# The gate of a decoder layer as seven block products per pair of tiles, its weight sums and the embedding product made during the up projection

## The chip, the cores and the metric

One core of a Trainium2 chip. The metric is the device time of one execution in microseconds; the median of three runs of the kernel before is 2149.36 us (2148.55 to 2155.91).

## The reference, cut to what matters

One layer over a prompt of 2048 rows and a sample group of 64 rows, D = 1024, all in float32. After the mixer come the feed-forward part and the gate:

```python
hf = rmsnorm(x, g_pre_mlp)
ff = jnp.square(jax.nn.relu(hf @ w_up)) @ w_down       # 1024 -> 4096 -> 1024
x = x + rmsnorm(ff, g_post_mlp)
gate = jax.nn.sigmoid(x @ w_ple_gate + b_ple_gate)     # 1024 -> 1024
x = x + gate * (pe @ w_ple)                            # pe: 256 columns per row
```

The change is in the last two lines and in where their parts are made.

## The kernel before, in words

Rows are worked on in 16 tiles of 128 (t = 0 to 15) and one of 64 for the sample group (t = -1). Each float32 operand of a product is split in two parts of a narrower float type, the high part by a cast on ACT and the low part as the difference on VectorE (`split_into`, L205 to L208, `lo_of`, L129), and each product of 128 x 128 by 128 x 512 is three matmuls: high by high, high by low, low by high (`mm3`, L132).

Four stages follow one another, and TensorE goes through them in this order:

1. The mixer (attention, pooling, output projection), to about 610 us; it also writes the first residual's rows to DRAM (`x1d`).
2. The up projection, to about 1267 us. Rows are taken in pairs of tiles, which makes a product of 2 x 2 blocks, done by Strassen's scheme in Winograd's form: seven block products in place of eight (`UpQuad`: p1, p2, p6, p7, p5 and two in `end`). Sums of blocks of the rows and of the weights are formed first (`a_sums`, L848; `up_weights`, L1004). 3 blocks of 352 columns by 16 slices of the weights are 48 rounds; `ahead` (L1150) loads and splits the weights of the next round. In block 0 VectorE also forms the weight differences, which go to DRAM (`upt`) for the other two blocks.
3. The down projection (`down_quads`, L1368), to about 1903 us: 8 groups of weights by 8 pairs of tiles, again seven products each; the sums of rows and weights are made on GpSimd, and the products are added on VectorE to 17 tiles `zs` that stay in SBUF. In the last group the places for weights that come free take the first of the gate's weights.
4. The gate, tile by tile (`gate`, L1447; the order is 0, 1, the sample, 2 to 15). `second_residual` (L1201) of the tile after: the sum of squares on ACT, two one-column operations on GpSimd, scaling and addition of `x1d` on VectorE, eight transposes on TensorE into a PSUM bank, split out of that bank. Then for each half of 512 columns 8 block products (24 matmuls) with the split gate weights that lie in SBUF and 2 (6 matmuls) of the embedding. The end of a half:

```python
V.tensor_tensor(out=y, in0=pg[:n], in1=bgate[:n, oc], op=ALU.add)
A.activation(out=y, in_=y, func=AF.Tanh, scale=0.5)
V.scalar_tensor_tensor(out=y, in0=y, scalar=1.0, in1=pl[:n, cs], op0=ALU.add, op1=ALU.mult)
V.scalar_tensor_tensor(out=y, in0=y, scalar=0.5, in1=zs[t][:n, oc], op0=ALU.mult, op1=ALU.add)
SY.dma_start(yr[:, oc], y)
```

`pg` and `pl` are PSUM banks. The last half of the last tile is done in two pieces of 256 columns, so that less is left after the last matmul.

The order of the instructions of each engine is fixed when the kernel is built: a scheduler takes them in the order of the program, lets one go ahead of another by what it reckons of their times, and each engine then runs its own list in order. `products` (L945) sets the order of the program in stages 2 and 3: p1 of a pair, then the last two products (`end`) of the pair before, then p2, p6, p7, p5; `ahead` and `then` hang other work on these steps. All transfers are issued from one queue, SP's, in order. PSUM has six banks for products (`acc`) and two for transposes (`trb`). Tiles in SBUF come from rings of places: `raws` (4 and one more, 4 KB a partition), `wr` (10, 8 KB), `turned8` (3, 8 KB).

Of the kernel before, what the change touches and what calls it, by code (L numbers as in the profile page):

```python
# [51 lines left out]
UP_N = 352  # L52

# [35 lines left out]
def trunk(ctx: ExitStack, tc: tile.TileContext, i: dict, o: dict):  # L89
# [728 lines left out]
    with ExitStack() as sb:  # L818
# [27 lines left out]
        x1d = {t: dp.tile([P, D], F32, name=f"x1d{t + 1}") for t in range(-1, NT)}  # L846

# [118 lines left out]
        with ExitStack() as s3:  # L966
# [36 lines left out]

            def up_weights(b, j):  # L1004
# [105 lines left out]
            def up_rounds():  # L1110
# [36 lines left out]
                for k, r in enumerate(rounds):  # L1147
                    quads = [UpQuad(*r[0], o7s[r[0][0]], held.pop(k))]

                    def ahead(k=k, b=r[-1][0], j=r[-1][1]):  # L1150
                        begin(1) if k == 0 else prepare(k + 1)
                        if j == DFF // 256 - 2 and b + 1 < N_BLOCKS:
                            o7s[b + 1] = load_ops(b + 1)
# [13 lines left out]
        zs = {t: zp.tile([P, D], F32, name=f"z{t + 1}") for t in range(-1, NT)}  # L1167
# [12 lines left out]
        def gate_unit(load):  # L1180
            raw = raws.tile([P, 2, 512], F32)
            queue(raw, load.rearrange("(k p) f -> p k f", p=P))
            return wtile(raw)

        wgs, wps = {}, {}

        def gate_weights():

            for nh in range(2):
                ns = slice(nh * 512, nh * 512 + 512)  # L1190
                for u in range(4):
                    wgs[u, nh] = gate_unit(w_gate[u * 256 : (u + 1) * 256, ns])
                    yield
                wps[nh] = gate_unit(w_ple[:, ns])
                yield

        gate_loads = gate_weights()

        gpost = None

        def second_residual(t):  # L1201

            m = turned8.tile([P, 2, 8, P], F32R)
            n = tn(t)
            z = zs[t]
            xt = raws.tile([P, D], F32)
            SY.dma_start(xt[:n], x1d[t][:n])
            rs = sumsq(few, z[:n], n, m.rearrange("p a c n -> p (a c n)")[:, :D])
            V.scalar_tensor_tensor(out=z[:n], in0=z[:n], scalar=rs[:n], in1=gpost[:n], op0=ALU.mult, op1=ALU.mult)
            V.tensor_tensor(out=z[:n], in0=xt[:n], in1=z[:n], op=ALU.add)  # L1210
            for j in range(2):
                ps = trb.tile([P, 4, P], F32, tag="tr", name="trx")
                for c in range(4):
                    T.transpose(ps[:, c, :n], z[:n, (4 * j + c) * P : (4 * j + c + 1) * P], ident[:n, :n])
                js = slice(4 * j, 4 * j + 4)
                lo = m[:, 1, js] if t >= 0 else m[:, 0, js, NS:]
                A.copy(out=m[:, 0, js, :n], in_=ps[:, :, :n])
                lo_of(lo, ps[:, :, :n], m[:, 0, js, :n])
            return m

        with ExitStack() as s4:
# [48 lines left out]
            class DownQuad:  # L1270
# [51 lines left out]
                def end(self):  # L1322
# [3 lines left out]
                    self.add(self.z, 1, 0)  # L1326

# [40 lines left out]
            def down_quads():  # L1368
# [4 lines left out]
                def quad(k):  # L1373
# [3 lines left out]
                    def ahead():  # L1377
# [15 lines left out]
                        else:  # L1393
# [3 lines left out]
                            if 2 <= tp <= 4:  # L1397
                                next(gate_loads)
                            if tp == 3:
                                fold_sample()  # L1400

# [14 lines left out]
                def more(k, tile=None):  # L1416
                    for _ in islice(gate_loads, k):
                        pass
                    if tile is not None:
                        normed[tile] = second_residual(tile)  # L1420

                r.then = {"p2": lambda: more(2, 0), "p6": lambda: more(1), "p7": lambda: more(1), "p5": lambda: more(1)}
                yield [q, r]

            normed = {}
# [3 lines left out]
        with ExitStack() as s5:  # L1429
            p5 = pool(s5, "p5")  # L1430

            def embedding(t):
                n = tn(t)
                c0 = t * P if t >= 0 else SEQ
                pt = p5.tile([P, 2, P], F32, tag="pt", bufs=2, name="pt")
                SY.dma_start(pt[:, :, :n], p_t[:, :, c0 : c0 + n])
                pe = p5.tile([P, 2, 2, P], F32R, tag="pe", bufs=2, name="pe")
# [95 lines left out]
```

## Time and profile before

| | |
|---|---|
| runs, us | 2148.55, 2155.91, 2149.36 |
| span of the profiled execution, us | 2152.2 |
| device time of that very execution | not listed apart from the runs |
| granted TensorE clock, mean | 0.994 |
| matmuls in the program | 11439 |
| moved by DMA | 320.43 MB, 149 GB/s over the span |

How to read the profile: PE is TensorE's matmuls, PEld its weight loads, DVE VectorE, ACT ScalarE, POOL GpSimd, SP the engine that issues transfers. A group of instructions is shown by line, engine, operation, output and inputs and their shapes; then the count, its busy time, the mean in ns, the idle time of the engine just before it and what ended that. A row of the timeline begins with start and duration in us. Matmuls of a stream overlap in the records: the duration of one is longer than the distance to the next.

### The profile page before, as it was taken

The numbers are of one execution on the slowest core, as the hardware profiler recorded it, in microseconds if no ns is written. First come the engines' busy times: TensorE is split into PE (matmuls) and PEld (weight loads), VectorE is DVE, ScalarE is ACT, GpSimd is POOL, SyncE is SP. The second block draws the span as 40 slices with busy tenths as digits, with TensorE's granted clock in tenths as the row PEclk, the third lists the DMA queues.
The fourth block names the chain that finished last, engine by engine and source line by source line (L and its number), as shares of the span: only waits on it lengthen the run. The fifth ranks groups of instructions, "written<-read, shape, count | busy, mean of one in ns | idle before, by whom it ended". The sixth has DMA issues, their size and how long they took to land.

```text
span 2152.2 us, 31209 instructions
## 1 busy us (share of the span) xinstructions
PE 2130.7 (99%) x11439; PEld 1884.6 (88%) x11439; DVE 1572.5 (73%) x2719; ACT 958.2 (45%) x1864; POOL 569.4 (26%) x643
## 2 busy tenths in 40 slices
PE   8999999999999999999999999999999999999999
PEld 6888888788889999999999988888888888888887
DVE  6799888876678777555755577888888888876553
ACT  4667666545555446444544455232233233232221
POOL 2334334343440000000000046434434444300000
PEclk9999999999999999999999999999999999999999
DMA  7552222768789768666766632231231322342211
GB/s 219 169 184 80 75 62 74 265 216 235 237 248 315 239 216 276 203 191 191 229 194 187 182 112 78 91 121 51 93 96 53 98 93 71 106 138 83 89 54 40
DMA packets 310007, 320.43 MB, mean 149 GB/s; under 512 B 79775, under 2 KB 257247, under 8 KB 302654
## 3 DMA queue, kind: packets, MB, share of 16 engines
q1 hardware_dynamic: 309854, 318.44, 47.1%
q8 instruction: 90, 1.47, 0.3%
q14 instruction: 63, 0.52, 0.1%
HBM read 217.17 MB, written 102.51 MB: 149 GB/s over the span
## 4 chain that ended last, share of the span: by engine, by line
PE 90%; DMA 3%; POOL 2%; issue 2%; ACT 2%; DVE 2%; SPq 0%; ACTq 0%; POOLq 0%; DVEq 0%
PE up L1056 10%; PE up L1058 10%; PE up L1057 10%; PE dn L1289 9%; PE dn L1287 9%; PE dn L1288 9%; PE pg L136 3%; PE pg L135 3%; PE pg L134 3%; PE qps L136 1%; PE ups L134 1%; PE qps L134 1%; PE ups L136 1%; PE ups L135 1%; PE qps L135 1%
## 5 line engine op out<-in xcount | busy, mean ns | idle before, releaser
L1297 DVE TENSOR_TENSOR z<-dn,z 128x512 f32<-128x512 f32 x416 | 280.4, 685 | 86.1 <-PE dn L1289 78.9
L130 DVE TENSOR_TENSOR g<-raw,g 128x512 fp32r<-128x512 f32 x336 | 226.1, 694 | 82.9 <-ACT g L207 82.4
L1056 PE MATMUL up<-e,g 128*128 128x352 f32 x832 | 269.4, 324 | 5.4 <-ACT snap L1063 5.4
L1057 PE MATMUL up<-e,g 128*128 128x352 f32 x832 | 267.9, 322 | 0.0
L1058 PE MATMUL up<-e,g 128*128 128x352 f32 x832 | 264.0, 323 | 0.0
L207 ACT CAST g<-raw 128x512 fp32r<-128x512 f32 x336 | 203.2, 623 | 90.1 <-PE up L1058 80.8
L1236 POOL TENSOR_TENSOR raws<-raws 128x1024 f32<-128x1024 f32 x32 | 80.0, 2504 | 595.7 <-DVE wr L130 407.9
L1288 PE MATMUL dn<-wr,ms 128*128 128x512 f32 x512 | 199.2, 389 | 0.0
L1287 PE MATMUL dn<-wr,ms 128*128 128x512 f32 x512 | 199.1, 389 | 0.0
L1289 PE MATMUL dn<-wr,ms 128*128 128x512 f32 x512 | 198.2, 389 | 0.0
L1056 PEld LDWEIGHTS up<-e,g 128*128 128x128 f32 x832 | 156.6, 188 | 6.6 <-ACT snap L1063 6.5
L1070 DVE TENSOR_TENSOR t<-up,snap 128x352 f32<-128x352 f32 x144 | 71.2, 520 | 120.3 <-ACT snap L1063 101.8
L1057 PEld LDWEIGHTS up<-e,g 128*128 128x128 f32 x832 | 157.4, 189 | 0.1
L1058 PEld LDWEIGHTS up<-e,g 128*128 128x128 f32 x832 | 156.0, 189 | 0.0
L1288 PE MATMUL dn<-wr,m 128*128 128x512 f32 x384 | 149.4, 389 | 0.0
L1287 PE MATMUL dn<-wr,m 128*128 128x512 f32 x384 | 149.4, 389 | 0.0
L1289 PE MATMUL dn<-wr,m 128*128 128x512 f32 x384 | 149.4, 389 | 0.0
L207 ACT CAST m<-fr 128x512 fp32r<-128x512 f32 (+1 forms) x128 | 65.5, 514 | 185.2 <-PE dn L1289 167.6
L1063 ACT COPY snap<-up 128x352 f32<-128x352 f32 x144 | 61.0, 455 | 175.0 <-PE up L1058 174.9
L849 POOL TENSOR_TENSOR s<-fr 128x256 f32<-128x256 f32 x64 | 49.5, 774 | 334.7 <-DVE ms L130 252.8
L207 ACT CAST wr<-raws 128x1024 fp32r<-128x1024 f32 x66 | 69.1, 1051 | 122.8 <-PE dn L1289 58.8
L141 POOL TENSOR_SCALAR rst<-ss 128x1 f32<-128x1 f32 (+1 forms) x68 | 25.3, 372 | 340.1 <-ACT ms L183 211.4
(279 smaller groups left out, 5798.8 us busy)
## 6 DMA issues: line engine op xcount, KB each, us to landing
raw<-in_w_up_dram SPq DMA_DIRECT2D x160, 256.0 KB, 5.0
raw<-upt SPq DMA_DIRECT2D x32, 1024.0 KB, 7.8
fr<-ffd SPq DMA_DIRECT2D x64, 512.0 KB, 3.6
ffd<-r SPq DMA_DIRECT2D x96, 256.0 KB, 2.6
upt<-raw SPq DMA_DIRECT2D x16, 1024.0 KB
raws<-in_w_down_dram SPq DMA_DIRECT2D x32, 512.0 KB, 5.5
sp<-hfd SPq DMA_DIRECT2D x21, 704.0 KB, 6.5
xt<-in_x_t_dram SPq DMA_DIRECT2D x16, 512.0 KB, 7.2
```

The source lines that it names most:

```text
L130: eng.tensor_tensor(out=out, in0=full, in1=hi.bitcast(F32), op=ALU.subtract)
L134: T.matmul(ps, lhs[0], rhs[0], start=first, stop=False)
L135: T.matmul(ps, lhs[0], rhs[1], start=False, stop=False)
L136: T.matmul(ps, lhs[1], rhs[0], start=False, stop=last)
L207: copy(out=dst[:, 0], in_=src)
L1056: T.matmul(ps, l[0], r[0], start=st, stop=False, skip_group_check=not fresh)
L1057: T.matmul(ps, l[0], r[1], start=False, stop=False, skip_group_check=not fresh)
L1058: T.matmul(ps, l[1], r[0], start=False, stop=c == 3, skip_group_check=not fresh)
L1287: T.matmul(ps, l[0], r[0], start=fresh and j == 0, stop=False, skip_group_check=not fresh)
L1288: T.matmul(ps, l[0], r[1], start=False, stop=False, skip_group_check=not fresh)
L1289: T.matmul(ps, l[1], r[0], start=False, stop=j == 1, skip_group_check=not fresh)
L1297: V.tensor_tensor(out=z, in0=ps, in1=z, op=ALU.add)
```

## The change

- **The gate** goes by pairs of tiles, seven block products of 4 x 3 matmuls each (`GateQuad`), in the order of pairs 0, 6, 7, 1, 2, 3, 4, 5; the sample (`GateSample`) comes second, with four products of block rows as before. `products` sets the order here as well. The sums of a pair's blocks are made on GpSimd (`gate_sum_operands`), and the first and third partial sums are copied out of PSUM on ACT and get the bias on GpSimd (`snap`).
- **The gate's weights**: four differences, formed on GpSimd, and seven splits of them are made during the up projection (`gate_sums`) and go to DRAM as `gwd`; 14 loads of 1 MB bring them back, from the last down group on.
- **The embedding product** with its factor 0.5 is also made during the up projection (`embeddings`), into the banks of `trb`, and goes to DRAM (`pld`); the gate reads it from SBUF.
- `ahead` of the up projection takes two steps of these two (`aside`) in every round after round 2.
- **The rows**: the 16 tiles `zs` become a ring `zr` of eight pairs. Pairs 1 to 5 are written to DRAM (`zd`) when their last down product is added, and their places take gate weights and row sums; they come back one by one in the gate (`load`). The addition of the first residual moves to GpSimd, but for the pair 6; its rows from `x1d` go through one place of `raws` for both tiles.

The diff, cut:

```diff
+SPILLED = (1, 2, 3, 4, 5)
+GATE_ORDER = (0, 6, 7, 1, 2, 3, 4, 5)
...
+            def gate_sums(st):
+                gw = pool(st, "gw")
+                for c in range(4):
+                    raw = gw.tile([P, 7, 512], F32, tag="raw", bufs=1, name="graw")
+                    b11, b21, t2, t3, t1, b22, t4 = (raw[:, k] for k in range(7))
+                    for dst, r, h in ((b11, 0, 0), (t3, 0, 1), (b22, 1, 1), (b21, 1, 0)):
+                        SY.dma_start(dst, w_gate[r * 512 + c * P : r * 512 + c * P + P, h * 512 : h * 512 + 512])
+                    yield
+                    for t, x, y in ((t1, t3, b11), (t2, b22, t1), (t3, b22, t3), (t4, b21, t2)):
+                        G.tensor_tensor(out=t, in0=x, in1=y, op=ALU.subtract)
+                    yield
+                    for k in range(7):
+                        w = gw.tile([P, 2, 512], F32R, tag="w", bufs=1, name="gw")
+                        split_into(w, raw[:, k], A.copy)
+                        yield
+                        SY.dma_start(gwd[k][c // 2][:, :, c % 2], w.bitcast(F32))
...
+                    ps = trb.tile([P, 512], F32, tag="tr", name="pl")
+                    for c in range(2):
+                        mm3(ps[:n], (pe[:, 0, c, :n], pe[:, 1, c, :n]), (w[:, 0, c], w[:, 1, c]), c == 0, c == 1)
+                    out[k] = ep.tile([P, 512], F32, tag="pl", bufs=2, name="plo")
+                    A.mul(out=out[k][:n], in_=ps[:n], mul=0.5)
+                    store(k - 1)
+                    yield
...
                         begin(1) if k == 0 else prepare(k + 1)
+                        for _ in islice(aside, 2 if k > 2 else 0):
+                            pass
...
+        def second_rows(t, junk, add=G, xt=None):
             n = tn(t)
             z = zs[t]
+            if xt is None:
+                xt = first_rows(t)
+            rs = sumsq(few, z[:n], n, junk)
             V.scalar_tensor_tensor(out=z[:n], in0=z[:n], scalar=rs[:n], in1=gpost[:n], op0=ALU.mult, op1=ALU.mult)
-            V.tensor_tensor(out=z[:n], in0=xt[:n], in1=z[:n], op=ALU.add)
+            add.tensor_tensor(out=z[:n], in0=xt[:n], in1=z[:n], op=ALU.add)
...
+        def gate_sum_operands(tp, h, s, s23, s14, a22):
+            (a11, a12), (a21, b22) = halves(h[0]), halves(h[1])
+            s1, s2 = next(s), next(s)
+            G.tensor_tensor(out=s1, in0=a21, in1=b22, op=ALU.add)
+            G.tensor_tensor(out=s2, in0=s1, in1=a11, op=ALU.subtract)
+            split_into(s23[:, :, 0:4], s2, A.copy)
+            split_into(s14[:, :, 0:4], s1, A.copy)
+            s3 = next(s)
+            G.tensor_tensor(out=s3, in0=a11, in1=a21, op=ALU.subtract)
+            split_into(s23[:, :, 4:8], s3, A.copy)
+            G.tensor_tensor(out=s2, in0=a12, in1=s2, op=ALU.subtract)
+            split_into(s14[:, :, 4:8], s2, A.copy)
+            a22 = a22()
+            split_into(a22, b22, A.copy)
...
+                    if self.g == DFF // 512 - 1 and self.tp in SPILLED:
+                        SY.dma_start(zd[self.tp], pair_rows[self.tp])
...
+                def snap(self, ps):
+                    s = self.place()
+                    with tc.high_priority():
+                        A.copy(out=s, in_=ps)
+                    G.tensor_tensor(out=s, in0=s, in1=self.bias(0), op=ALU.add)
+                    return s
+                def plus(self, out, ps, s):
+                    with tc.high_priority():
+                        V.tensor_tensor(out=out, in0=ps, in1=s, op=ALU.add)
+                def out(self, h, c, y, cs=slice(0, 512)):
...
+                    A.activation(out=y, in_=y, func=AF.Tanh, scale=0.5)
+                    V.scalar_tensor_tensor(out=y, in0=y, scalar=1.0, in1=self.pl[h ^ c][:, h, cs], op0=ALU.add, op1=ALU.mult)
+                    V.tensor_tensor(out=y, in0=y, in1=zs[t][:, oc], op=ALU.add)
+                    SY.dma_start(yp[t * P : t * P + P, oc], y)
...
+                    def p5(i=i):
+                        if i + 1 < n:
+                            next_sums(q[i + 1])
+                        if i + 2 < n:
+                            both(q[i + 2])
+                    quad.then = {"p5": p5}
+                    if i + 2 < n:
+                        quad.then["p2"] = lambda i=i: load(i + 2)
+                    if i + 1 < n:
+                        quad.then["p6"] = lambda i=i: next_turn(q[i + 1], 0)
+                        quad.then["p7"] = lambda i=i: next_turn(q[i + 1], 1)
+                    yield [quad]
```

`next_turn` transposes a tile's rows (eight transposes, copies on ACT) and for the first tile of a pair splits them; `both` is `second_rows` for both tiles of a pair.

353 lines of the change are left out of this document (270 added, 83 removed).

## The prediction

> **What bounds the kernel now.** I read the page first, then the busy time by stretches, the waits of TensorE, the chain of waits, and last the groups by line with single stretches of the timeline. The page:
>
> ```profile
> span 2152.2 us, 31209 instructions
> PE 2130.7 (99%) x11439; PEld 1884.6 (88%) x11439; DVE 1572.5 (73%) x2719; ACT 958.2 (45%) x1864; POOL 569.4 (26%) x643
> PE 90%; DMA 3%; POOL 2%; issue 2%; ACT 2%; DVE 2%; SPq 0%; ACTq 0%; POOLq 0%; DVEq 0%
> ```
>
> TensorE is busy 99% of the span and carries 90% of the chain. By stretches (columns: stretch, its length, then busy us of PE, PEld, DVE, ACT, POOL, the granted clock, DMA share, GB/s): block 0 of the up projection, the last down group, the gate, and two up rounds early in block 0. The last line is the whole of TensorE's waits after 620 us.
>
> ```profile
> 620.00:835.00 215.00, 214.46 (x1333) 213.93 (x1333) 166.21 (x277) 105.59 (x204) 11.62 (x8) 0.99 0.79 255
> 1800.00:1898.00 98.00, 98.00 (x434) 80.66 (x433) 82.03 (x113) 30.24 (x39) 29.79 (x36) 1.00 0.31 97
> 1990.00:2120.00 130.00, 130.00 (x612) 108.34 (x611) 71.04 (x100) 30.92 (x61) 5.94 (x16) 1.00 0.19 65
> 654.00:667.60 13.60, 13.60 (x87) 13.60 (x86) 11.86 (x18) 8.59 (x17) 0.00 (x0) 1.00 1.08 328
> 667.60:681.80 14.20, 13.66 (x85) 13.37 (x85) 8.46 (x17) 3.85 (x9) 0.00 (x0) 1.00 1.04 360
> PE up L1056 <- ACT snap L1063: 5.4, 3, 4.3
> ```
>
> So from the up projection to the end TensorE waits 5.4 us in all. A matmul taken out is worth its whole time, a matmul moved to another stage is worth nothing, and every wait that the change adds in front of TensorE is lost in full.
>
> **What it takes from TensorE.** Two pieces of the chain of waits, one tile apart in the gate, and the group that counts its products:
>
> ```profile
> 1974.16 0.87 PE trx L1214 x8
> 1988.67 0.87 PE trx L1214 x8
> L134 PE MATMUL pg<-wr,ms 128*128 128x512 f32 x248 | 97.6, 394 | 0.0
> L134 PE MATMUL pl<-wr,pe 128*128 128x512 f32 x64 | 24.9, 389 | 0.0
> ```
>
> A tile takes 1988.67 - 1974.16 = 14.51 us and holds 48 gate matmuls, 12 of the embedding and 8 transposes: (14.51 - 0.87) / 60 = 0.2273 us a matmul, 0.109 a transpose (the 394 ns of a group is pipelined time, not spacing). The gate has 3 x 248 of full width and, with the halved last piece, 768 in full widths. Seven products of 4 x 3 for 8 pairs are 672. **96 fewer x 0.2273 = 21.8 us less.** The sample's 32, all transposes and 204 embedding matmuls stay; those 3 x 64 and the sample's 12 move (46 us) into the up projection, where TensorE is as full: nothing. A pair then takes 84 x 0.2273 + 16 x 0.109 = 20.8 us of TensorE.
>
> **What the gate's other engines must do in those 20.8 us.** This decides the case, since before GpSimd had 5.94 us of work in 130. A full round (outputs of one pair, sums of the next, rows of the one after) needs, on GpSimd: 4 sums and 2 bias additions of 512 columns, 2 row additions of 1024, and 2 x 2 one-column operations. On VectorE, operations with both inputs in SBUF: 8 for the outputs (the embedding product now comes from SBUF instead of PSUM) and 5 low parts of 512, one low part of 1024 and two row scalings of 1024. The five additions out of PSUM stand apart. Prices, the nearest rows (min/median/max ns in the first two):
>
> ```profile
> L411 POOL TENSOR_TENSOR qr<-qr,rb x17: 1277/1295/4388, 23.3 to 379.9; 128x512 f32<-128x512 f32 x16, 64x512 f32<-64x512 f32 x1
> L1236 POOL TENSOR_TENSOR raws<-raws x32: 2394/2402/3263, 1057.1 to 1805.9; 128x1024 f32<-128x1024 f32 x32
> 2003.17 0.19 POOL L141 TENSOR_SCALAR rst<-ss 128x1 f32<-128x1 f32 x1 [13.68 <-ACT ms L183]
> 2003.44 0.55 POOL L143 TENSOR_TENSOR rsq<-rst,small 128x1 f32<-128x1 f32 x1
> 1412.68 1.22 DVE L130 TENSOR_TENSOR wr<-raws,wr 128x1024 fp32r<-128x1024 f32 x1
> 1413.81 0.68 DVE L1297 TENSOR_TENSOR z<-dn,z 128x512 f32<-128x512 f32 x1
> 1414.41 0.68 DVE L130 TENSOR_TENSOR m<-fr,m 128x512 fp32r<-128x512 f32 x1
> 1415.01 1.22 DVE L130 TENSOR_TENSOR ms<-s,ms 128x1024 fp32r<-128x1024 f32 x1
> L1209 DVE SCALAR_TENSOR_TENSOR z<-z,rsq,raws 128x1024 f32<-128x1024 f32 x16 | 20.5, 1279 | 0.6 <-POOL rsq L143 0.6
> ```
>
> From start to next start VectorE takes 0.60 for 512 columns and 1.13 for 1024. GpSimd: 6 x 1.29 + 2 x 2.40 = 12.5. VectorE: 13 x 0.60 + 1.13 + 2 x 1.28 = 11.5. Each alone fits in 20.8. But they don't run beside each other:
>
> ```profile
> 539.88 1.28 DVE L881 SCALAR_TENSOR_TENSOR z<-xt,rsq,g_pre_mlp 128x1024 f32<-128x1024 f32 x1 [0.72 <-POOL rsq L143]
> 541.08 2.32 DVE L130 TENSOR_TENSOR ms<-mr,ms 128x1024 fp32r<-128x1024 f32 x1
> 540.05 2.27 POOL L851 TENSOR_TENSOR s<-h 128x512 f32<-128x512 f32 x1 [0.20 <-ACT h L894]
> 542.29 2.27 POOL L849 TENSOR_TENSOR s<-h 128x512 f32<-128x512 f32 x1
> 544.63 1.29 POOL L850 TENSOR_TENSOR s<-s,h 128x512 f32<-128x512 f32 x1
> 547.59 1.93 POOL L143 TENSOR_TENSOR rsq<-rst,small 128x1 f32<-128x1 f32 x1
> L1297 DVE TENSOR_TENSOR z<-dn,z 128x512 f32<-128x512 f32 x416 | 280.4, 685 | 86.1 <-PE dn L1289 78.9 <-ACT z L1295 4.1
> ```
>
> L851 takes 2.27 instead of 1.29 and ends 1.16 after L881 does; L130, begun at 541.08, takes 2.32 instead of 1.22 and ends 1.08 after L851; L849 ends 1.16 after L130. They take turns, each for its whole length; even a one-column operation waits (L143: 1.93 instead of 0.55). The addition from PSUM, L1297, has 0.685 in the mean of 416 beside a busy GpSimd: it takes no part. So in a full round the two demands add: 12.5 + 11.5 = 24.0 us against 20.8, and 25.5 if the four one-column operations (2 x 0.74) count.
>
> The page "SBUF — State Buffer" of the Trainium skill, section "Who interferes with whom", states this as a rule: VectorE with two SBUF inputs and a GpSimd operation that reads SBUF share a port that is locked for a whole instruction. The rows above agree, and by the rule the sum of the gate is the one worked out here from them.
>
> Five rounds are full, and the start is fuller: round 0 and the sample need the rows of two pairs. The last deadline is the third product of the last pair, which needs its sums. Before it TensorE has 644 matmuls and 120 transposes, 146.4 + 13.1 = 159.5 us. The shared work due: rows of the first pair, on VectorE, 2 x 1.28 + 2 x 1.13 = 4.8; of six pairs 6 x (2.56 + 4.80) = 44.2; sums and splits of seven 7 x (5.16 + 3.0 + 1.13) = 65.0; 27 outputs x 1.2 = 32.4; 15 bias additions 19.4; the sample about 6.9. That is 172.7: 13.2 late. With the one-column operations (7 x 1.48) it is 23.6; with six outputs put off behind the deadline, 6. I take 14, since the two have little to do in the first microsecond and a one-column operation moves almost nothing. **Gate: 14 us given back, ends 6 and 24.**
>
> **The up projection.** 16 differences of 512 columns on GpSimd (11.62 us busy of 215), 28 casts on ACT (105.59 of 215) with 28 low parts on VectorE (166.21 of 215): at two steps a round, 1.6 splits and so 1.1 us of VectorE in 13.4. That is covered once the weights lead by a round. They don't at first: the change starts in round 3, just where the two rounds quoted have a DMA share of 1.08 and 1.04 at 328 and 360 GB/s. Rows that bear on it, the last four on loads into the gate:
>
> ```profile
> ACT g L207 <- DMA raw<-in_w_up_dram: 8.2, 6, 3.6
> ACT wsp L762 <- DMA wod<-wsp: 9.8, 7, 3.3
> raw<-upt SPq DMA_DIRECT2D x32, 1024.0 KB, 7.8
> wo<-wod SPq DMA_DIRECT2D x8, 1024.0 KB, 11.1
> fr<-ffd SPq DMA_DIRECT2D x64, 512.0 KB, 3.6
> xt<-in_x_prompt_dram SPq DMA_DIRECT2D x16, 512.0 KB, 5.6
> ```
>
> One MB of gate weights and up to three stores of 0.5 MB at 0.34 MB/us are 7 us in which the up weights may come late. The second wait is new: one buffer for the split, so that each cast on ACT waits for the store before it, and behind it on ACT stand the snaps that TensorE needs. L762 has that pattern: 9.8 us in 16, so 17 in 28 on ACT, of which a snap meets a small part. SP's queue gets 28 + 34 stores that wait for VectorE or ACT; behind them stand loads with a round of lead. Bounds 0 and 10, and no gain, since TensorE waits for nothing here that could go; **3**, nearer to the 5.4 us that TensorE waits now in the whole stretch.
>
> **The down projection.** The splits of the gate's weights go, the rows of three tiles, one pair's sums and five stores of 1 MB come; TensorE is busy 98.00 of 98.00 there and waits for neither: 0. The last three MB of gate weights can only be loaded when the last down products release their place, and are due 5 products, 13.6 us, into the gate. One MB lands in 7.8, in a queue of eight in 11.1: hidden, **1**, ends 0 and 5.
>
> **The end.** As before, two half-width pieces and four steps behind each, but the output before them is now on VectorE as well: **0.5**, ends 0 and 1.
>
> ```profile
> 2147.36 0.28 PE L136 MATMUL pg<-wr,ms 128*128 128x256 f32 x1
> 2149.04 0.42 DVE L1477 SCALAR_TENSOR_TENSOR y<-y,z 128x256 f32<-128x256 f32 x1
> ```
>
> **Sum.** -21.8 + 14 + 3 + 1 + 0.5 = -3.3 us. The profiled execution spans 2152.2 us, between the runs shown (2148.55 to 2155.91), 2.8 over their median; its own time outside the span isn't given, so I take the difference over to the median: 2149.4 - 3.3 = **2146 us**. This case alone reaches from 2134 (gate 6, up projection 0) to 2162 (gate 24, up projection 9).
>
> **Rivals.** First, the gain stays: the sums have a round of lead, and the scheduler puts VectorE's outputs where GpSimd is idle. For it: in the last down group VectorE and GpSimd have 82 and 30 us in 98 and TensorE never waits. Against it: most of that 82 is L1297, which doesn't share. Then -21.8 + 3 + 0.5 = **2131** (2128 without the 3).
>
> Second, slower, by one loop, for which two more rows count:
>
> ```profile
> L894 ACT COPY h<-trx 128x512 f32<-128x512 f32 x32 | 18.3, 582 | 0.0
> L207 ACT CAST g<-raw 128x512 fp32r<-128x512 f32 x336 | 203.2, 623 | 90.1 <-PE up L1058 80.8 <-DMA raw<-in_w_up_dram 8.2 <-ACT g L207 0.8
> ```
>
> Both tiles' first-residual rows go through one buffer, so the second row addition waits for the first and then for a load; the next pair's sums wait for that addition and the transposes. Sums 5.2, addition 2.4, load of 512 KB 3.6 to 5.6, addition 2.4, transposes 0.9, two copies 1.2: 16 to 18. The third sum waits for the split of the first (two small buffers), two casts and a low part: 2 more. Seven GpSimd operations can each meet one of VectorE's of 0.60 to 1.28: 4 to 9. That is 22 to 29 a round. At 29 five rounds lose 41: 2149.4 - 21.8 + 41 + 3.5 = **2172**. It decides from 26.4 a round, where 5 x 5.6 = 28 uses up the gain and 0.5% more. Against it: the first addition can go ahead of the sums.
>
> Third, that the change doesn't do what it says: the products are plainly written out 7 a pair, so no chance is kept for it.
>
> **Chances.** My forecast 0.50, the gain stays 0.33, the loop 0.17. 0.5% is 10.7 us, about what a measurement of this kernel can tell from no change: faster is below 2138.6, slower above 2160.1. The gain staying is faster; of the forecast 0.07 lies below 2138.6 and 0.01 above 2160.1. Faster 0.33 + 0.07 = 0.40, same 0.42, slower 0.17 + 0.01 = 0.18. Cases of both signs hold most, so the range reaches from within the first rival, 2129, to the forecast's upper end, 2162: it leaves out the loop, 0.17, and little else.
>
> **What would show it.** In the stretch of the gate's middle rounds: a pair every 24 to 25 us instead of 20.8, TensorE waiting for a transpose (rows late) or the third product (sums late), GpSimd's 512-column sums well over 1.29 us. Right if TensorE's waits in the gate sum to 6 to 24 us; wrong if they are below 3 (the first rival), or if the time is lost in the up projection behind late weights or snaps.

## The result, and the profile after

The changed kernel takes 2188.25 us (2180.20 to 2192.52, 4 runs) against 2149.87 of the kernel before: the ratio is 1.0167, with an interval of 1.0140 to 1.0194. It is slower by 38 us in the medians, where 3 us less were forecast, and it lies outside the range. The profiled execution is one of 2192.52 us, 4.3 over the median. Its page:

```profile
span 2190.6 us, 31570 instructions
PE 2130.6 (97%) x11331; PEld 1871.6 (85%) x11331; DVE 1658.3 (76%) x2766; ACT 1029.3 (47%) x2003; POOL 721.7 (33%) x724
PE 77%; DVE 8%; DMA 5%; issue 4%; POOL 3%; ACT 2%; SPq 0%; DVEq 0%; ACTq 0%; POOLq 0%
```

TensorE carried 90% of the chain and carries 77 now; VectorE's share went from 2% to 8, DMA's from 3 to 5 and GpSimd's from 2 to 3. Busy times by stretches, after: block 0 of the up projection, 85 us of the last two down groups, and everything from the sample's last down product to the end, which is most of the last down group with the gate.

```profile
620.00:835.00 215.00, 212.44 (x1318) 210.72 (x1318) 183.94 (x291) 114.15 (x220) 28.63 (x18) 0.99 0.91 299
1815.00:1900.00 85.00, 85.00 (x376) 69.87 (x375) 71.29 (x95) 25.90 (x36) 40.47 (x42) 1.00 0.38 122
1892.80:2190.60 297.80, 257.14 (x1117) 201.53 (x1115) 225.94 (x248) 102.24 (x177) 151.57 (x111) 0.95 0.48 167
```

The last of these stretches in the kernel before:

```profile
1844.30:2152.20 307.90, 303.34 (x1429) 251.43 (x1427) 188.18 (x265) 78.17 (x140) 23.53 (x47) 1.00 0.25 84
```

Before, TensorE was busy for 303.34 of 307.90 us. The prediction takes 46.4 (moved) and 21.8 (gone) from that, which leaves 235.1 of work and 239.7 of time. After has 297.80: **58.1 lost in this stretch**. TensorE's idle time went from 4.6 to 40.7 us, 36.1 more. Its busy time is 257.14 instead of 235.1, 22.0 more, at a granted clock of 0.95 instead of 1.00. The up projection grew from 658.1 to 709.2 us, by the 46.4 moved and 4.7 more. The mixer, which the change doesn't touch, differs between profiled executions by up to 8 us (601.9 to 609.8 over the kernels below), so I compare stretches as well as medians.

TensorE's waits after 620 us (total, times, longest); there was one line before, 5.4 us. The list lacks one wait of 4.4 us for a snap that ends at 616.9; its like before, 4.3, ended at 619.8 and is in the 5.4:

```profile
PE pg L1639 <- ACT y L1653: 14.3, 6, 5.9
PE pg L1641 <- DVE z L134: 6.0, 4, 3.2
PE dn L1404 <- DVE z L1414: 4.3, 3, 3.5
PE pg L1641 <- DVE ms L134: 4.2, 1, 4.2
PE pg L1639 <- DVE y L1659: 3.0, 3, 1.7
PE up L1142 <- ACT snap L1149: 1.8, 3, 1.0
PE trx L1317 <- POOL z L1309: 1.7, 1, 1.7
PE up L1144 <- DVE g L134: 1.3, 2, 0.7
```

The largest is the copy of a partial sum out of PSUM on ScalarE (L1653): the next product adds into the same bank and can't begin before it. TensorE waits for no gate weights. How a copy of 0.6 us comes to be late by 5.9 is read from the timeline of one stretch (start, duration, line, and in brackets the idle time before and what ended it), VectorE's rows first, then GpSimd's, ScalarE's and TensorE's:

```profile
2048.31 0.68 DVE L1659 TENSOR_TENSOR y<-pg,y 128x512 f32<-128x512 f32 x1
2048.91 3.48 DVE L134 TENSOR_TENSOR z<-s,z 128x512 fp32r<-128x512 f32 x2
2052.32 2.32 DVE L1308 SCALAR_TENSOR_TENSOR z<-z,rsq,raws 128x1024 f32<-128x1024 f32 x1
2054.56 1.77 DVE L1666 SCALAR_TENSOR_TENSOR y<-y,raws 128x512 f32<-128x512 f32 x1
2056.36 2.93 DVE L1667 TENSOR_TENSOR y<-y,z 128x512 f32<-128x512 f32 x1
2059.21 0.68 DVE L1659 TENSOR_TENSOR y<-pg,y 128x512 f32<-128x512 f32 x1
...
2061.70 1.29 DVE L1666 SCALAR_TENSOR_TENSOR y<-y,raws 128x512 f32<-128x512 f32 x2
2062.91 0.68 DVE L1659 TENSOR_TENSOR y<-pg,y 128x512 f32<-128x512 f32 x1
...
2049.04 2.81 POOL L1309 TENSOR_TENSOR z<-raws,z 128x1024 f32<-128x1024 f32 x1
2051.81 1.75 POOL L1654 TENSOR_TENSOR y<-y,b_ple_gate 128x512 f32<-128x512 f32 x1
2053.52 2.26 POOL L1332 TENSOR_TENSOR s<-h,s 128x512 f32<-128x512 f32 x1
2056.34 2.40 POOL L1309 TENSOR_TENSOR z<-raws,z 128x1024 f32<-128x1024 f32 x1 [0.56 <-DVE y L1666]
...
2059.92 0.63 ACT L1665 ACTIVATE y<-y 128x512 f32<-128x512 f32 x1 [10.27 <-DVE y L1659]
...
2063.62 0.63 ACT L1665 ACTIVATE y<-y 128x512 f32<-128x512 f32 x1 [1.52 <-DVE y L1659]
2064.16 0.57 ACT L1653 COPY y<-pg 128x512 f32<-128x512 f32 x1
...
2064.78 0.80 PE L1639 MATMUL pg<-wr,ms 128*128 128x512 f32 x1 [5.90 <-ACT y L1653]
```

From 2048.9 to 2059.2 every VectorE operation reads two tiles of SBUF, and each lasts until GpSimd gives way: 2.93 for an addition that takes 0.68 alone. The addition at 2059.21, L1659, reads PSUM and isn't slowed itself (0.68), but it stands behind them. ScalarE's tanh waits 10.27 us for it. The copy L1653 comes later in ScalarE's list, behind two more tanhs; the last of these waits another 1.52 us for the addition that VectorE reaches at 2062.91. TensorE waits 5.90 us for the copy. Of the six waits for this copy, four (12.6 of the 14.3 us) have a tanh that waited for VectorE right ahead of the copy; this is the longest of them. Then comes a second price, in stretches of TensorE just behind that wait:

```profile
2064.80:2070.00 5.20, 5.20 (x17) 4.32 (x18) 4.11 (x4) 2.67 (x4) 1.72 (x1) 0.52 0.60 197
2070.00:2076.00 6.00, 6.00 (x28) 4.86 (x27) 1.38 (x2) 1.79 (x5) 2.59 (x2) 1.00 0.56 223
```

For 5.2 us the clock is granted at 0.52: 17 instructions where 28 fit into 6.0 us afterwards; matmuls start 0.43 us apart instead of 0.23. The Trainium skill, page "TensorE: Matmul & The Clock Gate", section "Part 1: The HAM clock gate (the "warmup" mystery)", says that the array falls to half its clock after an idle window of about 3.4 us. The clock of 0.52 behind a wait of 5.90 agrees; but it fell behind a wait of 2.02 as well (last section), so 3.4 us is no floor here. In the last stretch 49 matmuls are 0.36 to 0.46 apart, 9.6 us over the usual 0.227. The other 12 of the 22 us are not shown to come from the clock: the kernel e12 below, at a granted clock of 1.00, also has 240.25 us of busy time where the count leaves 235.1, so about 5 of them come without it, and 7 stay open.

The last down group shows the same hold:

```profile
1911.30 2.89 POOL L1309 TENSOR_TENSOR zsample<-raws,zsample 64x1024 f32<-64x1024 f32 x1
1914.15 1.25 POOL L1325 TENSOR_TENSOR raws<-raws 128x512 f32<-128x512 f32 x1
...
1912.62 3.87 DVE L134 TENSOR_TENSOR z<-raws,z 128x1024 fp32r<-128x1024 f32 x1 [0.68 <-ACT z L211]
1916.41 3.27 DVE L1414 TENSOR_TENSOR z<-dn,z 128x512 f32<-128x512 f32 x5
```

One low part, 1.22 us alone, is held through two GpSimd operations for 3.87, and five additions of down products out of PSUM come in a row behind it; TensorE waits 3.5 us for a bank (L1404 in the list of waits).

### The profile page after: what moved, and what is told of

The parts are those of the page before. It is cut to its first block, busy times and chain, and to the rows that moved or that the text cites. A ratio compares the mean times of both kernels' runs of the same rounds, so it can differ in the third digit from the quotient of the medians.

```text
span 2190.6 us, 31570 instructions
## 1 busy us (share of the span) xinstructions
PE 2130.6 (97%) x11331; PEld 1871.6 (85%) x11331; DVE 1658.3 (76%) x2766; ACT 1029.3 (47%) x2003; POOL 721.7 (33%) x724
## 4 chain that ended last, share of the span: by engine, by line
PE 77%; DVE 8%; DMA 5%; issue 4%; POOL 3%; ACT 2%; SPq 0%; DVEq 0%; ACTq 0%; POOLq 0%
PE up L1142 9%; PE up L1144 9%; PE up L1143 9%; PE dn L1404 9%; PE dn L1406 9%; PE dn L1405 9%; DMA z<-zd 1%; PE qps L140 1%; PE ups L138 1%; PE qps L138 1%; PE ups L140 1%; PE qps L139 1%; PE ups L139 1%; PE trp L552 1%; DVE y L1666 1%
## 5 line engine op out<-in xcount | busy, mean ns | idle before, releaser
L134 DVE TENSOR_TENSOR g<-raw,g 128x512 fp32r<-128x512 f32 x336 | 236.2, 720 | 97.7 <-ACT g L211 85.4
L1404 PE MATMUL dn<-wr,ms 128*128 128x512 f32 x512 | 200.1, 392 | 4.0 <-DVE z L1414 4.0
L1404 PE MATMUL dn<-wr,m 128*128 128x512 f32 x384 | 150.1, 391 | 0.4 <-DVE z L1414 0.3
L211 ACT CAST ms<-s 128x1024 fp32r<-128x1024 f32 (+1 forms) x78 | 75.9, 973 | 103.0 <-PE dn L1406 55.6
L1404 PEld LDWEIGHTS dn<-wr,ms 128*128 128x128 f32 x512 | 96.6, 189 | 25.0 <-DVE z L1414 3.9
```

Source lines behind the costliest of these rows:

```text
L134: eng.tensor_tensor(out=out, in0=full, in1=hi.bitcast(F32), op=ALU.subtract)
L211: copy(out=dst[:, 0], in_=src)
L1404: T.matmul(ps, l[0], r[0], start=fresh and j == 0, stop=False, skip_group_check=not fresh)
```

## The experiments

The theory, P: VectorE and GpSimd take turns wherever both read SBUF, and in each engine's fixed list what stands behind waits with it. The rivals: the reload of the spilled rows is late (R); the loop over the one place for the first residual's rows (L, the prediction's second rival); VectorE simply has too much work (V); the copy's place in ScalarE's list (C); others stand with their runs. The table has for each kernel the median, the ratio to the kernel before on the same chip, the time of a round (a quarter of the time between the start of the 201st and the 537th of the gate's 716 matmuls, that is from the third pair to the seventh; TensorE needs 20.8), and the stretch from the sample's last down product to the end (239.7 would be all of the gain). Rounds named in the expectations were counted between transposes, whose place in the round differs by kernel, so they deviate by up to 3 us. Rounds and stretches are those of one profiled execution each, which can lie off its kernel's median: 6.8 us over it in e3, 4.1 under it in e16, 4.0 under it in e12. After's own interval is plus or minus 6 us wide: a kernel that lies less than that below after is told from it by its rounds and its last stretch, if at all.

| kernel | median, us | ratio [interval] | round | last stretch |
|---|---|---|---|---|
| after | 2188.25 | 1.0167 [1.0140, 1.0194] | 27.5 | 297.8 |
| e1_rows_dve | 2159.76 | 1.0043 [1.0027, 1.0060] | 25.3 | 269.6 |
| e2_bias_dve | 2178.04 | 1.0135 [1.0120, 1.0150] | 25.9 | 281.5 |
| e4_rows_bias_dve | 2163.72 | 1.0069 [1.0054, 1.0084] | 24.2 | 269.7 |
| e5_all_dve | 2151.55 | 1.0011 [1.0002, 1.0020] | 21.7 | 261.8 |
| e3_sums_dve | 2182.41 | 1.0152 [1.0133, 1.0170] | 27.0 | 293.0 |
| e6_sum_in_place | 2156.00 | 1.0030 [1.0021, 1.0039] | 22.6 | 263.1 |
| e7_last_add_pool | 2199.39 | 1.0232 [1.0217, 1.0247] | 28.8 | 306.4 |
| e10_idle_reads | 2189.78 | 1.0187 [1.0169, 1.0204] | 27.0 | 295.5 |
| e11_idle_memsets | 2158.27 | 1.0039 [1.0024, 1.0053] | 22.5 | 264.3 |
| e12_first_copy | 2145.76 | 0.9975 [0.9965, 0.9986] | 21.5 | 253.8 |
| e13_squares_ready | 2184.20 | 1.0155 [1.0139, 1.0172] | 27.4 | 294.6 |
| e14_bias_add_dve | 2190.64 | 1.0183 [1.0154, 1.0212] | 28.3 | 298.3 |
| e15_copy_dve | 2182.08 | 1.0151 [1.0134, 1.0168] | 26.4 | 292.6 |
| e16_sums_squares | 2177.94 | 1.0126 [1.0110, 1.0142] | 25.3 | 284.6 |
| e17_rows_dve_reads | 2177.62 | 1.0128 [1.0112, 1.0143] | 27.7 | 287.8 |
| e18_rows_halves | 2186.50 | 1.0170 [1.0153, 1.0187] | 27.5 | 292.7 |

**Taking work from GpSimd.** e1_rows_dve:

```diff
-        def second_rows(t, junk, add=G, xt=None):
+        def second_rows(t, junk, add=V, xt=None):
```

> The row additions of the gate and of the last down group go from GpSimd to VectorE, nothing else. Theory P (VectorE with two SBUF inputs and GpSimd take turns): the shared demand of a full round falls from 24.0 us to 24.0 - 2 x 2.40 + 2 x 1.13 = 21.5, still over 20.8, so about 15 to 25 us of the 38 lost come back: 2165 to 2173 us. Rival Q (the order in ACT's queue alone: the copy out of PSUM stands behind an output's tanh, whatever the port does): VectorE has 2.3 us more per pair, the tanh waits longer: 2188 or up to 10 slower. Rival D (the rows read back from DRAM come late): within 5 us of 2188.

2159.8 us, 28.5 less than after; more than P's number, and in its direction. e2_bias_dve:

```diff
-                    with tc.high_priority():
-                        A.copy(out=s, in_=ps)
-                    G.tensor_tensor(out=s, in0=s, in1=self.bias(0), op=ALU.add)
+                    self.plus(s, ps, self.bias(0))
```

> The two partial sums are taken out of PSUM by VectorE, with the bias added in the same operation, instead of a copy on ACT and an addition on GpSimd. Theory P: the shared demand falls by 2 x 1.29 to 21.4 (an addition out of PSUM does not share): 2165 to 2173 us. Rival Q: TensorE no longer waits for anything on ACT there, so most of the loss goes: 2145 to 2155 us. Rival D: within 5 us of 2188.

2178.0, 10 less (the round 25.9 instead of 27.5): less than P said, and Q misses by more. e4_rows_bias_dve has both edits:

> Both together. Theory P: shared demand 24.0 - 2.54 - 2.58 = 18.9 us in 20.8, GpSimd has 5.2 and VectorE about 18.0 a round: the loss goes nearly all, 2132 to 2145 us. Rival Q: no better than the bias alone, since VectorE has 2.3 us a pair more. Rival D: within 5 us of 2188.

2163.7, a miss: the round is shorter than with the rows alone (24.2 against 25.3), but the last stretch as a whole isn't (269.7 and 269.6), since the start of the gate takes back what the rounds give. The median's 4 us over e1 are not the gate's: in the profiled executions the mixer takes 609.6 us in e4 and 605.0 in e1. e5_all_dve adds the four sums:

```diff
-            G.tensor_tensor(out=s1, in0=a21, in1=b22, op=ALU.add)
-            G.tensor_tensor(out=s2, in0=s1, in1=a11, op=ALU.subtract)
+            V.tensor_tensor(out=s1, in0=a21, in1=b22, op=ALU.add)
+            V.tensor_tensor(out=s2, in0=s1, in1=a11, op=ALU.subtract)
...
-            G.tensor_tensor(out=s3, in0=a11, in1=a21, op=ALU.subtract)
+            V.tensor_tensor(out=s3, in0=a11, in1=a21, op=ALU.subtract)
...
-            G.tensor_tensor(out=s2, in0=a12, in1=s2, op=ALU.subtract)
+            V.tensor_tensor(out=s2, in0=a12, in1=s2, op=ALU.subtract)
```

> The four sums on VectorE as well: GpSimd has only the one-column operations in the gate. Theory P: nothing is shared any more, but VectorE alone has 18.0 + 4 x 0.6 = 20.4 us in 20.8: 2135 to 2155 us, waits of TensorE now for VectorE. Rival Q: slower than with the two alone by the longer waits of the tanh. Rival D: within 5 us of 2188.

2151.6: VectorE alone does in 21.7 us a round what the two engines did in 27.5. e3_sums_dve has the sums' part alone:

> The changed kernel with the four sums of a pair's blocks on VectorE instead of GpSimd; rows and biases stay on GpSimd. Theory P (the two engines take turns at operations that read SBUF): GpSimd's 4 x 1.29 become VectorE's 4 x 0.60, so 24.0 us of shared work a round become 21.2; the middle round about 23 to 24.5 us in place of 27.6, and 2163 to 2174 us. Rival S (the sums have a round of lead and their engine doesn't matter; what counts is GpSimd's row additions of 2.4 us and the bias in the chain of the partial sums): 2182 to 2192 us.

2182.4: P misses, S holds in its number, and the interval meets after's. The parts don't add up: the sums alone give 6 us at most, and 12 when rows and bias have gone before.

**Putting reads on GpSimd.** e7_last_add_pool gives it more of the work (after, with the last addition of each output there):

```diff
-                    V.tensor_tensor(out=y, in0=y, in1=zs[t][:, oc], op=ALU.add)
+                    G.tensor_tensor(out=y, in0=y, in1=zs[t][:, oc], op=ALU.add)
```

> The changed kernel with the last addition of each output moved from VectorE to GpSimd: more for the shared part, less for VectorE. Theory P (they take turns): shared demand of a full round up by 4 x 1.29 - 4 x 0.60 = 2.8 us, a middle round 30 to 31 us instead of 27.6, 2198 to 2210 us. Rival V (VectorE's own load is what is too much): VectorE has 2.4 us less a round, 2170 to 2180 us.

2199.4: P's number, though the round, 28.8, is under its 30 to 31. Taking work from VectorE costs 11 us, so V falls. Two kernels do the whole work of e6 (below) and, beside it, work that nobody reads; they differ in whether GpSimd reads SBUF or only writes it. The nine reads or 21 memsets a tile, about as long on GpSimd, are issued behind the tile's last one-column operation (`lastq`) and write a tile of their own (`scr`):

```diff
+                with tc.issue_after(lastq[0].ins):
+                    for _ in range(9):
+                        G.tensor_tensor(out=scr, in0=bgate[:, 0:256], in1=bgate[:, 256:512], op=ALU.add)
```

```diff
+                with tc.issue_after(lastq[0].ins):
+                    for _ in range(21):
+                        G.memset(scr, 0.0)
```

> The version with the sum in place, and behind the one-column operations of each tile 9 additions of 256 columns on GpSimd that read SBUF and whose result nobody uses: about 13 us a round. Theory P: VectorE's 16 us a round with two inputs in SBUF and these 13 take turns: a middle round of 29 to 33 us instead of 20.9, 2190 to 2220 us. Rival R (only the wait for a result of GpSimd, or its queue, costs time): as with the memsets, 2140 to 2150 us.

> The same with 21 memsets of 256 columns instead of the 9 additions: as long on GpSimd, but they only write. Theory P: they do not share with VectorE's reads, a middle round stays near 21 us, 2138 to 2150 us. Rival R: the same time as with the additions, whichever it is.

2189.8 with the reads (two executions), a hair under P's range, with a round of 27.0, under its 29 to 33; this is 33.8 over e6. 2158.3 with the memsets (three executions), 8 over P's range, which took e6 to be faster than it is, but only 2.3 over e6, and the intervals of these two overlap; the rival R falls. The groups say where (count, busy us, mean ns). With the reads, in the gate:

```profile
L1670 DVE TENSOR_TENSOR y<-y,z 128x512 f32<-128x512 f32 (+1 forms) x33 | 29.1, 883 | 0.2
L1310 DVE SCALAR_TENSOR_TENSOR z<-z,rsq,raws 128x1024 f32<-128x1024 f32 x12 | 19.2, 1599 | 2.2 <-POOL rsq L149 2.1
L1662 DVE TENSOR_TENSOR y<-pg,y 128x512 f32<-128x512 f32 (+1 forms) x26 | 17.1, 663 | 1.1 <-PE pg L1646 1.0
```

With the memsets:

```profile
L1670 DVE TENSOR_TENSOR y<-y,z 128x512 f32<-128x512 f32 (+1 forms) x33 | 22.5, 686 | 0.2
L1662 DVE TENSOR_TENSOR y<-pg,y 128x512 f32<-128x512 f32 (+1 forms) x26 | 17.1, 665 | 0.9 <-PE pg L1646 0.8
L1310 DVE SCALAR_TENSOR_TENSOR z<-z,rsq,raws 128x1024 f32<-128x1024 f32 x12 | 15.4, 1282 | 9.5 <-POOL rsq L149 9.5
```

The additions of two SBUF tiles take 883 ns beside reads and 686 beside memsets, the scalings 1599 and 1282; the additions out of PSUM 663 and 665. VectorE's scalings wait less for GpSimd's one-column results beside the reads (2.1 us) than beside the memsets (9.5), so a longer queue on GpSimd isn't the price. This is P's mechanism by itself. The Trainium skill, page "SBUF — State Buffer", section "Who interferes with whom", says that VectorE with two inputs in SBUF contends with a GpSimd operation that reads SBUF and not with one that only writes it: the two kernels agree.

e17_rows_dve_reads and e18_rows_halves ask what it was in the row additions: e17 is e1 with three of those idle reads per tile; e18 is after with

```diff
-            add.tensor_tensor(out=z[:n], in0=xt[:n], in1=z[:n], op=ALU.add)
+            for c in (slice(0, 512), slice(512, D)):
+                add.tensor_tensor(out=z[:n, c], in0=xt[:n, c], in1=z[:n, c], op=ALU.add)
```

> The kernel with the row additions on VectorE (2159.8 us), and for each tile three additions of 256 columns on GpSimd beside them that read a tile which is always there (the bias) and write one that nobody reads: about the time, 3 x 0.77 us, that GpSimd's row addition took, without its place in any chain. Theory P (GpSimd's reads hold VectorE, whatever they are for): the gain goes back, 2178 to 2192 us. Theory L (the row addition on GpSimd cost its time in the loop over the one place for the first residual's rows: 2.4 us an addition there instead of 1.2): nothing of the kind is in the loop now, 2160 to 2169 us.

> The changed kernel with each row addition on GpSimd cut into two of 512 columns. Theory P by the sum of the work: 2 x (2 x 1.29 - 2.40) = 0.4 us a round more, 2185 to 2193 us. Rival H (what counts is how long one GpSimd operation holds a VectorE operation, and the PSUM additions queued behind it): 2168 to 2181 us.

e17 is 2177.6, at P's lower edge: 17.9 of e1's 28.5 us come back with reads whose results nobody waits for. L as the whole cause falls; up to 10.6 us may still be the loop's. Unlike in e10, GpSimd's sums and bias additions stand behind these reads in its list, and no memsets were set against them here, so a part of the 17.9 can be GpSimd's own time. e18 is 2186.5: H falls, the length of one hold isn't it.

**ScalarE's list.** Two kernels take the sums of squares of a tile that is always there: e13 in after, e16 in e3.

```diff
-            rs = sumsq(few, z[:n], n, junk)
+            rs = sumsq(few, gpost[:n] if t // 2 in SPILLED else z[:n], n, junk)
```

> The changed kernel, but the sum of squares of the rows of pairs 1 to 5 is taken of a tile that lies in SBUF (the gain) instead of the reloaded rows; the scale factor of these rows is another number, the work is the same. ScalarE then doesn't wait for the reload of the rows; VectorE's scaling does. In the changed kernel ScalarE waited 23.3 us in 5 times for the reloads, with casts and copies out of PSUM queued behind. Theory R (the late reload, through ScalarE's list, is a large part of the 58 us lost from the last down group on): 2160 to 2175 us. Theory P (VectorE and GpSimd taking turns sets the pace, and the reload is late because the outputs before it are): 2183 to 2191 us.

> The kernel with the four sums on VectorE (2182.4 us), and the sum of squares of the reloaded pairs' rows taken of the gain that lies in SBUF; the scale factor of these rows is another number. With the sums on VectorE the middle rounds stayed at about 27.9 us although 2.8 us of shared work a round had gone, and ScalarE waited up to 7.7 us for reloads with the casts of the sums behind it. If these waits took the gain of moving the sums: 2160 to 2172 us. If not, and GpSimd's row additions of 2.4 us hold the round: 2178 to 2186 us.

2184.2: R falls; the 4 us less lie within the intervals, and the round is the same (27.4). 2177.9, in neither range, a hair under the second; 4.5 less than e3, with intervals that overlap. The round is 25.3 instead of 27.0, but e3's profiled execution is its slowest and e16's its fastest. That the reloads took a part of what the sums had to give is likely and not settled. e14 and e15 part the edit of e2: in e14 only the bias addition goes to VectorE (`V.tensor_tensor` for `G.tensor_tensor`), in e15 only the copy (`V.tensor_copy(s, ps)` for `A.copy`).

> The changed kernel with the copy of the first and third partial sums on ScalarE as it was and only the bias addition on VectorE (both inputs in SBUF). It parts the gain of about 10 us that came when copy and bias became one VectorE addition out of PSUM. Theory P (the bias on GpSimd is the price): shared work falls by 2 x (1.29 - 0.60) = 1.4 us a round, 2176 to 2182 us. Rival C (the copy's place in ScalarE's list, behind activations that wait, is the price): 2185 to 2191 us, no gain.

> The other half: the copy of the partial sums out of PSUM on VectorE instead of ScalarE, the bias addition on GpSimd as it was. Rival C (the copy waits in ScalarE's list): 2175 to 2182 us. Theory P (the bias on GpSimd is the price, and VectorE has 1.2 us more of its own a round): 2186 to 2194 us.

2190.6 and 2182.1: C's numbers both times (the second a hair over its upper edge), P misses both, and the rounds go the same way, 28.3 and 26.4 against 27.5. The bias on GpSimd alone costs nothing that shows, and what e2 gained came with the copy; but the intervals of the three overlap, so this is a reading and not settled.

**The start of the gate.** In e5 TensorE still waits 6.96 us at 1961, for the third sum, whose place needs the first sum's split; VectorE has no idle time ahead of it, so its list can be the reason as well. e6_sum_in_place is e5 with

```diff
-            s3 = next(s)
-            V.tensor_tensor(out=s3, in0=a11, in1=a21, op=ALU.subtract)
-            split_into(s23[:, :, 4:8], s3, A.copy)
+            V.tensor_tensor(out=a21, in0=a11, in1=a21, op=ALU.subtract)
+            split_into(s23[:, :, 4:8], a21, A.copy)
```

> On top of the version with rows, bias and sums on VectorE: the third sum is written over the block it is taken from, so that it no longer waits until the first sum has been split into a place that waits for the store of pair 5's rows. If that store is the cause of the 7.0 us wait at the start of the gate, the wait and the half-speed matmuls behind it (15 at 0.43 instead of 0.23 us) go: 10 us less, 2139 to 2144 us. If it is the sums themselves that are late, no change: 2149 to 2154.

2156.0, neither number. The wait is there again, for something else; waits of TensorE at the start of the gate, then two rows of the timeline (SyncE's queue and VectorE):

```profile
PE pg L1638 <- DVE y L1656: 7.7, 1, 7.7
```

```profile
1961.57 0.33 SPq L182 DMA_DIRECT2D b_ple_gate<-in_b_ple_gate_dram  x1
...
1971.33 0.69 DVE L1656 TENSOR_TENSOR y<-pg,b_ple_gate 128x512 f32<-128x512 f32 x1 [0.53 <-DMA b_ple_gate<-in_b_ple_gate_dram]
```

The bias is loaded behind gate weights in the queue, 10 us late (in e5 it was issued at 1951.53), and now that the bias is added straight out of PSUM, TensorE's bank waits for it. e12_first_copy tests this: e6, and for the first pair alone

```diff
-                    self.plus(s, ps, self.bias(0))
+                    if self.tp == 0:
+                        with tc.high_priority():
+                            A.copy(out=s, in_=ps)
+                        V.tensor_tensor(out=s, in0=s, in1=self.bias(0), op=ALU.add)
+                    else:
+                        self.plus(s, ps, self.bias(0))
```

> All sums, biases and rows on VectorE and the third sum in place, as in the kernel of 2156.0 us, but for the first pair the first and third partial sums are again copied out of PSUM on ScalarE, and the bias is added on VectorE from SBUF. In that kernel TensorE stood 7.74 us at the start of the gate for the first bias addition out of PSUM, and that addition stood for the load of the bias, which was issued at 1961.57 us and over at about 1971. Theory L (the load of the bias holds the bank): the copy frees the bank, the 7.7 us and about 3 us of matmuls at half speed behind them go; 2144 to 2149 us, and no wait over 2 us at the start of the gate. Rival V (VectorE's list is late there whatever the bias does, because the four row scalings of the next two tiles stand ahead): a wait of 5 us or more stays at the start of the gate, at another bank; 2152 to 2158 us.

2145.8: the number of that expectation's L (the load), and TensorE's waits there are now 1.6 and 0.7 us.

```profile
PE pg L1638 <- DVE y L1661: 1.6, 1, 1.6
PE pg L1638 <- ACT y L1653: 0.7, 1, 0.7
```

That the copy alone would have done it, without the third sum in place, no run shows. This is the fastest kernel of the study, 4.8 us under the kernel before (2150.53 on that chip). The interval excludes 1, but the gain is half of the 0.5% that the prediction set as telling. Its last stretch:

```profile
1886.10:2139.90 253.80, 240.25 (x1117) 194.69 (x1115) 216.78 (x311) 97.29 (x163) 35.12 (x48) 1.00 0.55 196
```

14.1 us over the 239.7 that keep the whole gain, instead of after's 58.1, at a clock of 1.00. With 2.7 in the up projection (707.2 against 704.5) and 0.3 in the down groups, that is -21.8 + 14.1 + 2.7 + 0.3 = -4.7 from the up projection on, as measured.

## Why the prediction was wrong, step by step

**Right.** 96 matmuls less, 21.8 us, and the 46.4 moved for nothing: e12 is busy for 240.25 us where the count leaves 235.1, with few waits. The up projection: 3 was said, 4.7 came. Its waits rose from 5.4 to 7.5 us, counted from 600 us on:

```profile
PE up L1142 <- ACT snap L1149: 6.2, 4, 4.4
PE up L1144 <- DVE g L134: 1.3, 2, 0.7
```

These are the two places that the prediction feared, snaps on ScalarE and split weights, at 0.8 and 1.3 us more; the other 2.6 of the 4.7 I didn't divide. The gate's weights: 1 was said, and TensorE waits for none. That the two engines take turns was right (e10 and e11), and that the gate is decided by it as well (e5 leaves GpSimd only the one-column operations, and 36.7 of the 38.4 us go).

**Wrong: "Gate: 14 us given back, ends 6 and 24", and "the down projection: 0"**; together they are 58.1. The step that failed is "The five additions out of PSUM stand apart", with the sum "12.5 + 11.5 = 24.0 us against 20.8" made from it. They stand apart in that nothing slows them (663 ns beside reads). But they stand in VectorE's list, in order, behind operations that wait for GpSimd, as in the timeline above, and one that isn't next can't use GpSimd's turn. If none of them can, a round costs VectorE's whole list and GpSimd's reads: 24.0 and five additions at 0.60 are 27.0, or 28.5 with the one-column operations; measured were 27.5, where the prediction had 24.0. This sum was made behind the runs, and no run takes these additions out of VectorE's list: that they are the 3 us that were missing is argued from the timeline, not shown. So I held it against all runs, by the same prices and in the same two forms. It holds for e1 (24.5 to 26.0; 25.3), e2 (25.6 to 27.1; 25.9), e4 (23.1 to 24.6; 24.2), e5 and e12 (20.3 to 21.8; 21.7 and 21.5), e13, e16 and e18. It is 1.2 to 1.3 too low for e3 and e14, and 0.8 and 0.7 for e6 and e11. It is 1 to 2 too high where GpSimd got more or VectorE got the copy (e7, e15, e17), and 7 too high for the idle reads of e10. In e10 the prediction's own form, the contending parts alone, is nearer: 16.1 and 18 reads at 0.77 are 30.0 against 27.0. VectorE was busy for 97.81 of the 99.60 us from 2046.4 on there, so some of its work went on beside the reads; which part stays open. e15 has two more operations out of PSUM on VectorE and yet the shorter round (26.4). So it is a budget, not a law; e14 and e15, and e3 against e16, hint that the order of ScalarE's list counts as well.

With it the prediction's count to the last deadline, 172.7 us, becomes 172.7 + 10.4 for one-column operations + 20.4 for about 34 additions out of PSUM (27 outputs, five for every four) = 203.5, which is 44 late on 159.5, not 13.2. The rest has two sources that the prediction didn't price. The loss reaches TensorE through lists: it foresaw late rows and late third products, while the largest wait, 14.3 us, is for copies on ScalarE, most of it behind a tanh. And waits lower the clock: 22.0 us of the 58.1 are busy time, and 9.6 of them are shown to be matmuls at the lower clock. "The down projection: 0" was read from TensorE busy 98.00 of 98.00 without asking what the new GpSimd work does to the additions out of PSUM there. From the sample's last down product to the gate's first product TensorE has 259 matmuls in both kernels; after takes 64.4 us for them and e12 56.5, so about 8.

**The rivals.** "The gain stays" needed GpSimd idle whenever VectorE reads: no. "Slower, by one loop" has a time near the result, 2172, and its 22 to 29 us a round hold the 27.5; part of its working, GpSimd meeting VectorE, is the mechanism. But the loop as the whole cause is not borne out: TensorE waits for the row addition for 1.7 us, and idle reads move the time by 33.8 us (e10) and 17.9 (e17) with that addition on VectorE. What the loop adds, at most 10.6 us of e1, is open.

**Of what would show it:** GpSimd's sums took 1.5 to 1.9 us in the mean instead of 1.29, as said; a pair took 27.5, not 24 to 25; TensorE's waits in the gate sum to 31.6, over the 6 to 24.

## What to carry to other kernels

Where VectorE and GpSimd both read SBUF, budget a stage as one engine: all of VectorE's list, with what it does out of PSUM, and all of GpSimd's reads, and look at who stands behind a held operation in the list. Here the nearer end of this sum came within 2 us of the round in all kernels but e10, where it was 7 too high and the contending parts alone were nearer. Work moved to an idle GpSimd can cost more than it would on the busier VectorE: the same gate took 27.5 us a round shared and 21.7 on VectorE alone. When a wait has been removed, look for the load that is late next (here the bias) before calling the cause wrong.

## What the runs showed of the hardware that was not expected

- A VectorE operation can be held through two GpSimd operations in a row (3.87 us instead of 1.22): the turns aren't strictly one by one.
- GpSimd memsets, 288 of 0.31 us in the gate's records, cost 2.3 us in all, which the intervals don't tell from nothing; 126 additions that read SBUF cost 33.8.
- The clock falls behind some shorter waits too: behind a wait of 2.02 us at 2120.5 it was 0.57 for 3.3 us, behind one of 2.22 at 2090.7 it stayed at 1.00. It also stayed at 1.00 behind one of 2.46 at 2149.2, which had another of 1.66 only 4 us before it; what decides stays open.

```profile
2120.50:2123.80 3.30, 3.29 (x9) 2.57 (x10) 3.30 (x3) 0.13 (x1) 2.53 (x2) 0.57 0.21 79
2090.70:2097.00 6.30, 5.27 (x24) 3.60 (x24) 6.30 (x9) 3.10 (x6) 1.78 (x2) 1.00 0.66 216
2149.20:2156.00 6.80, 4.86 (x24) 3.76 (x24) 6.80 (x6) 3.06 (x5) 6.00 (x4) 1.00 0.46 154
```
